# Hybrid attention block: the gated norm's steps placed behind the next heads' scores, and one output gate tile placed ahead of the decays' sums

## The chip, the cores and the metric

The kernel runs on one core of one Trainium2 chip. The metric is the device time of one execution in microseconds (us); of several runs the median is given. TensorE is called PE here (its weight loads PEld), VectorE DVE, ScalarE ACT, GpSimd POOL and SyncE SP.

## The reference, cut to what matters

One layer of an encoder block over 512 positions of 1024 features, in float32: an RMS norm, one wide input projection, two mixers (multi-head latent attention and gated linear attention) that are gated and merged, and then a retrieval of experts by product keys, which takes up most of the time and which the change does not touch. The change touches the gated linear attention (GLA) and the place in the attention (MLA) into which its last steps are woven:

```python
log_a = jax.nn.log_sigmoid((gate_lr @ w_a2 + b_a2).astype(f32)) / GLA_TAU
cum = jnp.cumsum(log_a, axis=2)
cum_last = cum[:, :, -1]
k_dec = kc * jnp.exp(cum_last[:, :, None] - cum)
d_state = jnp.einsum('bclhk,bclhv->bchkv', k_dec, vc)
chunk_decay = jnp.exp(cum_last)
...
o = jnp.einsum('bclhk,cbhkv->bclhv', qc, states)
o = o * lax.rsqrt(jnp.mean(o * o, axis=-1, keepdims=True) + EPS) * g_gn.astype(f32)
o = o.reshape(B, S, H * dv) * jax.nn.silu(out_gate.astype(f32))
```

So each of the 4 GLA heads has decays (sums of log decays and their exponentials), an output that is divided by the root of its mean square (the gated norm), and an output gate. The attention has 8 heads: scores, a masked softmax, and the product with the values.

## The kernel before

Everything is held transposed: features on the 128 partitions, the 512 positions along the row. A product in full precision is made of three matmuls on split operands: high x high, low x high, high x low. A weight tile comes from memory as `raw`; ACT makes its high half `whi`, POOL (some times DVE) its low half `wlo = raw - whi`. The order on every engine is the order in which the program is written (`manual_schedule`); the engines run their own queues and meet at semaphores.

*Decays and gates (lines 536 to 559).* `la` holds the log decays. After two query tiles (`gq`), for each of the 4 blocks of 128 positions PE makes a sum (`pd`, in one of two banks called `pst`), ACT takes its exponential (line 546) and DVE multiplies it onto the keys (`kd`). Then 16 small matmuls give the chunks' totals and ACT their exponentials (`dec`, line 554). Then come 4 output gate tiles: each is 24 matmuls on a weight tile (`proj`, banks `pmm`), a DVE product with the row norm `rX`, and a Silu on ACT (line 559).

*The attention (loop at line 765), heads counted from 0.* One turn `hd` makes the scores of head `hd + 1` (`scores`: 4 matmuls into `pmm` banks; for each, DVE masks, takes the maximum into `stat` and scales it, and ACT takes the exponential into `x`), pieces of gate projections that fill PE's time (`fill`, `piece`: 3 matmuls a piece), the values of head `hd` (`values`: the probabilities of 4 blocks are transposed by PE into two banks called `pk`; DVE copies blocks 0 and 2 out, ACT blocks 1 and 3; then 4 matmuls), and the scaling of head `hd + 1`'s probabilities (`normalise`, DVE).

*The gated norm.* `gla_norm` (in turns 0 and 2, for two heads each) sums the squares by two matmuls; DVE scales the sums into `gsq` (trace name `t`, program name `t_1164`), and ACT makes r = exp(-0.5 ln) (`rB`). A Newton step and the scaling follow for each head: `gla_scale` makes u = -0.5 r r on DVE and u = u x gsq on POOL (line 613) and puts the rest, `gla_scaled`, on a list called `later`: r = (u + 1.5) r on DVE, and the product of the head's output `yb32` (trace name `t`, program name `t_960`) with r on POOL (line 619). `run()` issues all that is on the list. The steps of heads 0 and 1 stand in turns 1 and 2, those of heads 2 and 3 in turns 3 and 4.

Of the kernel before, what the change touches and what calls it, by code (L numbers as in the profile page):

```python
# [16 lines left out]
AF = mybir.ActivationFunctionType  # L17
OP = mybir.AluOpType
# [175 lines left out]
def body(ctx, tc, a, out):  # L194
    nc = tc.nc
    pe, act, dve, pool, sp = (Metered(nc.tensor, _pe_ns), nc.scalar, Metered(nc.vector, _dve_ns), nc.gpsimd, nc.sync)
# [55 lines left out]
    def run(n=1000):  # L252
        for _ in range(n):
            if later:
                later.pop(0)()

    def weights(key):

        while half:
            split_lo()  # L260
        while state["split"] < min(pos_of[key] + 2, len(queue)):
            split_one()
        run(1)
        return ready.pop(key)
# [50 lines left out]
    def pmm(name="pmm"):  # L315
        return ps.tile([128, T], F32, name=name, bufs=4 if name == "pmm" else 2)
# [5 lines left out]
    def tmp(dt=F32, n=T):  # L322
        return tp[0].tile([128, n], dt, name="tmp", bufs=tp[1])
# [80 lines left out]
    def proj(key, xs=None, bank="pmm"):  # L404
        w = weights(key)
        p = pmm(bank)
        acc(p if key[0] != "u" else p[:, GT:], pairs(w, NC_D), xs or hx)
        if key[0] != "u":
            further(key)
        return p  # L410
# [4 lines left out]
    rX = sb.tile([128, T], F32, name="r2")  # L415
# [73 lines left out]
    for c in range(NC_D):  # L489
# [28 lines left out]
        if c >= 3 and c - 3 < NT:  # L518
            tt = c - 3
            p = pmm("pst")  # L520
# [15 lines left out]
    sg, gq = sgq[:, 0:4], sgq[:, 4:6]  # L536
    kd = sb.tile([128, NT, 256], F32, name="kd")
    dec = fr.tile([128, 16], F32, name="dec")
    for i in range(2):
        p = proj(("w1", 6 + i))  # L540
        dve.scalar_tensor_tensor(gq[:, i], p, GDK ** -0.5, rX, op0=OP.mult, op1=OP.mult)
    for tt in range(NT):
        pd = pmm("pst")
        pe.matmul(pd[:, :256], tri, la[:, tt], start=True, stop=True)
        e = tmp(n=256)
        act.activation(e, pd[:, :256], AF.Exp)
        dve.scalar_tensor_tensor(kd[:, tt], pk[tt // 2][:, (tt % 2) * 256:(tt % 2) * 256 + 256], rcol[:, tt:tt + 1], e,
                                 op0=OP.mult, op1=OP.mult)
# [3 lines left out]
            pe.matmul(ptot[:, hp * 8 + 2 * tt:hp * 8 + 2 * tt + 2], la[:, tt, hp * 128:(hp + 1) * 128],  # L552
                      cc(C_IND, 2), start=True, stop=True)
    act.activation(dec, ptot[:, :16], AF.Exp)
    for i in range(4):
        p = proj(("w1", 8 + i))
        t = tmp()
        dve.tensor_tensor(t, p, rX, op=OP.mult)
        act.activation(sg[:, i], t, AF.Silu)


    st = fr.tile([128, 8, 2, 128], F32, name="t2")
# [46 lines left out]
    def gla_scale(hd):  # L609
        r = rg[hd]  # L610
        u = tmp()
        dve.scalar_tensor_tensor(u, r, -0.5, r, op0=OP.mult, op1=OP.mult)
        pool.tensor_tensor(u, u, gsqs[0][:, hd], op=OP.mult)
        later.append(lambda: gla_scaled(hd, u))
# [11 lines left out]
    for g in range(3):  # L626
        w = weights(("wq", g))
        for i in range(2):
            p = pmm()
# [5 lines left out]
            if g < 2:  # L635
                hd = 2 * (2 * g + i)
                act.activation(qT[0:64, hd], p[0:64], AF.Copy)
                dve.tensor_copy(qT[0:64, hd + 1], p[64:128])
            else:

                t, x = tmp(), tmp()
# [7 lines left out]
    for i in range(4):  # L649
        p = pmm()  # L650
# [14 lines left out]
    for tt in range(NT):  # L665
        ts = slice(tt * 128, (tt + 1) * 128)
        p = pmm()
# [13 lines left out]
    def scores(hd):  # L681
        pr = both[:, (hd % 2) * NT:(hd % 2 + 1) * NT]
        st4 = fr.tile([128, 16], F32, name="stat", bufs=3)
        probs[hd] = pr, st4
        for i in range(NT):
            n = (i + 1) * 128
            p = pmm()
            pe.matmul(p[:, :n], qT[0:96, hd, i * 128:n], kT[0:96, hd, :n], start=True, stop=True)
            dve.memset(p[0:64, n - 64:n], -1e30)
            mx, b, sm = (st4[:, 4 * j + i:4 * j + i + 1] for j in range(3))  # L690
            dve.reduce_max(mx, p[:, :n], axis=AX.X)
            dve.tensor_scalar(b, mx, -scale, None, op0=OP.mult)
            act.activation(pr[:, i, :n], p[:, :n], AF.Exp, bias=b, scale=scale, accum_out=sm)
            piece(FS[i] if hd else 0)
# [27 lines left out]
    def fill(n):  # L722
        while half:
            split_lo()
        while gpend:
            i, p = gpend.pop(0)
            t = tmp()
            dve.tensor_tensor(t, p, rX, op=OP.mult)
            sp.dma_start(gated[i], t)
        piece(n)  # L730
# [34 lines left out]
    for hd in range(MH):  # L765
        if hd + 1 < MH:
            scores(hd + 1)
        fill(FILL[1])
        if hd in (0, 2):
            run()  # L770
            gla_norm((hd, hd + 1))
        values(hd)
        if hd + 1 < MH:
            normalise(hd + 1)
        if hd in (1, 3):
            gla_scale(hd - 1)
        fill(FILL[2])
        if hd == 4:
            run()
            yb = [fr.tile([128, 4, T], F32R, name="t3"), fr.tile([128, 4, T], F32R, name="t4")]  # L780
        if hd >= 4:
            split(yb[0][:, hd - 4], yb[1][:, hd - 4], yb32[:, hd - 4], dve)
        elif hd % 2:
            run()
            gla_scale(hd)
        else:
            run()
    while gpend or half:
# [21 lines left out]
    for mt in range(8):  # L810
        g = []
        for s in range(2):
            i = 2 * mt + s
            if i in EARLY:
                t = gin.pop(i)
            else:
                p = proj(("w1", 12 + i))
                t = tmp()
# [6 lines left out]
        for s, y in ((1, yb), (0, ya)):  # L825
            p = pmm()
# [11 lines left out]
    for mt in range(8):  # L838
        p = proj(("wo", mt), mgx)
# [45 lines left out]
    hd = dr.tile([2, 128, D], F32, name="hd")  # L885
# [86 lines left out]
    for mt in range(16):  # L972
# [3 lines left out]
        p = proj(("wpq", mt), h2x)  # L976
# [488 lines left out]
```

## Time and profile before

| | us |
|---|---|
| median of 3 runs | 1633.83 (1633.63 to 1634.84) |
| profiled execution | 1642.5 |
| its span, first to last instruction | 1640.7 |
| PE busy | 1609.1 |
| DVE busy | 1242.6 |
| ACT busy | 728.5 |
| POOL busy | 355.2 |

The profile is one execution. Its rows give, for an instruction or several alike in a row, the start from the beginning of the span, the time it took, the engine, the line, the operation with its output and inputs and, in brackets, how long the engine stood idle before it and which engine's work on which tile ended that wait. Line 161 is that of a helper through which PE and DVE instructions pass; there the tiles tell what an instruction is. The granted clock is PE's, as a share of 2.4 GHz. Busy times of different engines overlap; matmuls of a row overlap too, so that the start of the next row says more than the sum of durations.

### The profile page before, as it was taken

To read this page: it belongs to the slowest core of one execution; us is meant where nothing else is said; L and a number is where in the kernel's file an instruction comes from. 1 tells how busy PE (TensorE), PEld (TensorE's weight loads), DVE (VectorE), ACT (ScalarE), POOL (GpSimd) and SP (SyncE) were. 2 spreads that over 40 slices of the span, in tenths; PEclk is the share of its full clock that TensorE was granted. 3 is DMA by queue.
4 is the path that set the end of the run, shared out by engine and by line. 5 is a ranking of instruction groups with operands and counts; after the bars stand their busy time and mean duration, and the time that the engine had idled before them with its cause. 6 is when DMAs were issued, how large, how long until landed. Compare 5 with 4: busy or idle time off the path is not lost.

```text
span 1640.7 us, 23200 instructions
## 1 busy us (share of the span) xinstructions
PE 1609.1 (98%) x8487; PEld 1399.0 (85%) x8487; DVE 1242.6 (76%) x2513; ACT 728.5 (44%) x1257; POOL 355.2 (22%) x258
## 2 busy tenths in 40 slices
PE   7999999999999999999999999999999999999998
PEld 6777656888889999999999999888888888888776
DVE  6634575343797989889889737787988888988885
ACT  5552544333333645545455544444444434444343
POOL 4342143445354100000001010111111111111110
PEclk9999999999999999999999999999999999999999
DMA  5222112442433678788789898999999999999994
GB/s 170 73 81 77 52 58 90 157 157 90 141 105 128 204 279 291 255 292 309 265 302 350 327 354 291 315 372 344 382 383 356 388 355 377 359 361 367 344 382 151
DMA packets 154610, 415.82 MB, mean 253 GB/s; under 512 B 12343, under 2 KB 87608, under 8 KB 136448
## 3 DMA queue, kind: packets, MB, share of 16 engines
q1 hardware_dynamic: 118048, 230.28, 40.4%
q0 software_dynamic: 19888, 139.23, 22.5%
q10 hardware_dynamic: 16560, 44.83, 7.3%
q8 instruction: 66, 1.08, 0.3%
q14 instruction: 48, 0.39, 0.1%
HBM read 361.60 MB, written 52.17 MB: 252 GB/s over the span
## 4 chain that ended last, share of the span: by engine, by line
PE 85%; issue 4%; DVE 4%; DMA 4%; ACT 1%; POOL 1%; SPq 0%; DVEq 0%; POOLq 0%; ACTq 0%
PE pmm L161 63%; PE pst L161 12%; PE pk L161 10%; DMA ga<-gad 2%; DVE tmp L161 1%; DMA vraw<-in_v 1%; DMA raw<-in_u 1%; POOL wlo L242 1%; DVE t L161 1%; DVE vlo L161 0%; DVE rows L161 0%; DVE rB L161 0%; ACT whi L236 0%; DMA raw<-in_w 0%; DVE gout L161 0%
## 5 line engine op out<-in xcount | busy, mean ns | idle before, releaser
L161 PE MATMUL pmm<-act_hi,whi 128*128 128x384 f32 (+1 forms) x1016 | 362.4, 357 | 9.7 <-ACT act_hi L331 9.3
L161 PE MATMUL pmm<-act_hi,wlo 128*128 128x384 f32 (+1 forms) x1016 | 354.1, 349 | 1.8 <-DVE wlo L161 1.8
L161 PE MATMUL pmm<-act_lo,whi 128*128 128x384 f32 (+1 forms) x1016 | 354.0, 348 | 0.5 <-DVE act_lo L161 0.5
L1023 POOL DMA_INDIRECT rows<-in_uv,gidx x128 | 130.4, 1019 | 889.9 <-DVE gout L161 847.7
L236 ACT ACTIVATE whi<-raw 128x1024 fp32r<-128x1024 f32 (+1 forms) x201 | 209.1, 1042 | 98.8 <-PE pmm L161 52.6
L242 POOL TENSOR_TENSOR wlo<-raw,whi 128x1024 fp32r<-128x1024 f32 (+1 forms) x79 | 186.1, 2360 | 244.8 <-ACT whi L236 234.8
L161 DVE TENSOR_TENSOR wlo<-raw,whi 128x1024 fp32r<-128x1024 f32 x122 | 148.8, 1222 | 88.7 <-ACT whi L236 87.0
L161 PEld LDWEIGHTS pmm<-act_hi,whi 128*128 128x128 f32 x1016 | 192.2, 189 | 24.2 <-ACT act_hi L331 9.3
L161 PEld LDWEIGHTS pmm<-act_hi,wlo 128*128 128x128 f32 x1016 | 192.0, 189 | 11.6 <-DVE wlo L161 2.4
L161 PE MATMUL pmm<-vlo,chi 128*128 128x512 f32 x512 | 200.0, 391 | 1.6 <-DVE vlo L161 1.5
L161 PE MATMUL pmm<-vhi,clo 128*128 128x512 f32 x512 | 199.3, 389 | 1.0 <-DVE clo L161 1.0
L161 PE MATMUL pmm<-vhi,chi 128*128 128x512 f32 x512 | 199.5, 390 | 0.9 <-ACT vhi L1279 0.9
L161 PEld LDWEIGHTS pmm<-act_lo,whi 128*128 128x128 f32 x1016 | 192.4, 189 | 9.0 <-DVE act_lo L161 1.0
L161 DVE SCALAR_TENSOR_TENSOR gout<-rows,gact,gout 128x1024 f32<-128x1024 f32 x128 | 163.9, 1281 | 0.0
L161 DVE TENSOR_TENSOR vlo<-vraw,vhi 128x1024 fp32r<-128x1024 f32 x128 | 156.0, 1219 | 4.4 <-ACT vhi L1279 4.4
L1279 ACT ACTIVATE vhi<-vraw 128x1024 fp32r<-128x1024 f32 x128 | 134.2, 1050 | 49.8 <-DMA vraw<-in_v 49.1
L161 DVE SCALAR_TENSOR_TENSOR rows<-rows,hrep 128x1024 f32<-128x1024 f32 x128 | 155.9, 1218 | 0.0
L161 PE MATMUL pmm<-t,whi 128*128 128x512 f32 x436 | 138.6, 399 | 0.0
L161 PEld LDWEIGHTS pmm<-vlo,chi 128*128 128x128 f32 x512 | 96.1, 188 | 24.3 <-DVE vlo L161 4.5
L1035 ACT ACTIVATE gact<-gact 128x1 f32<-128x1 f32 x128 | 25.9, 202 | 199.1 <-DVE rows L161 198.9
L161 PEld LDWEIGHTS pmm<-vhi,clo 128*128 128x128 f32 x512 | 96.1, 188 | 20.3 <-DVE clo L161 1.5
L161 PEld LDWEIGHTS pmm<-vhi,chi 128*128 128x128 f32 x512 | 96.1, 188 | 19.9 <-ACT vhi L1279 1.3
(276 smaller groups left out, 2785.9 us busy)
## 6 DMA issues: line engine op xcount, KB each, us to landing
raw<-in_u SPq DMA_DIRECT2D x128, 512.0 KB, 5.4
vraw<-in_v SPq DMA_DIRECT2D x124, 512.0 KB, 8.4
gt<-gd SPq DMA_DIRECT2D x30, 768.0 KB, 10.3
gd<-gs ACTq DMA_DIRECT2D x11, 2048.0 KB, 8.1
gad<-gx ACTq DMA_DIRECT2D x96, 192.0 KB, 5.1
ga<-gad SPq DMA_DIRECT2D x95, 192.0 KB, 9.6
raw<-in_w SPq DMA_DIRECT2D x28, 512.0 KB, 3.3
raw<-in_wpq SPq DMA_DIRECT2D x16, 512.0 KB, 3.5
```

The source lines that it names most:

```text
L161: return f(*args, **kw)
L236: act.activation(hi[:, :n], raw[:, :n], AF.Copy)
L242: (lo_eng or lo_home[0]).tensor_tensor(lo[:, :n], raw[:, :n], hi[:, :n], op=OP.subtract)
L1023: pool.indirect_dma_start(out=rows[n], out_offset=None, in_=a["uv"], in_offset=bass.IndirectOffsetOnAxis(ap=gidx[:, n:n + 1], axis=0))
L1035: act.activation(g, g, AF.Gelu)
L1279: act.activation(hi, vraw[n], AF.Copy)
```

## The change

The function `gate_out` holds one output gate tile; tile 0 is now made before the decays' sums and tiles 1 to 3 after them. In the attention, the steps of the gated norm leave the ends of turns 1, 3 (and what remained of them in turns 2 and 4) and stand in turns 2 and 4 right behind the scores of the next head, both heads of a pair at once: `gla_scale`, `run()`, `gla_scale`, `run()`.

```diff
+    def gate_out(i):
+        p = proj(("w1", 8 + i))
+        t = tmp()
+        dve.tensor_tensor(t, p, rX, op=OP.mult)
+        act.activation(sg[:, i], t, AF.Silu)
+
+    gate_out(0)
     for tt in range(NT):
         pd = pmm("pst")
         pe.matmul(pd[:, :256], tri, la[:, tt], start=True, stop=True)
...
     act.activation(dec, ptot[:, :16], AF.Exp)
-    for i in range(4):
-        p = proj(("w1", 8 + i))
-        t = tmp()
-        dve.tensor_tensor(t, p, rX, op=OP.mult)
-        act.activation(sg[:, i], t, AF.Silu)
+    for i in range(1, 4):
+        gate_out(i)
...
         if hd + 1 < MH:
             scores(hd + 1)
+        if hd in (2, 4):
+            gla_scale(hd - 2)
+            run()
+            gla_scale(hd - 1)
+            run()
         fill(FILL[1])
...
         if hd + 1 < MH:
             normalise(hd + 1)
-        if hd in (1, 3):
-            gla_scale(hd - 1)
         fill(FILL[2])
...
             split(yb[0][:, hd - 4], yb[1][:, hd - 4], yb32[:, hd - 4], dve)
-        elif hd % 2:
-            run()
-            gla_scale(hd)
         else:
             run()
```

On ACT at the decays (`kd` is still the log decays' work tile, `x_726` the Silu's output, `tmp<-pst` the exponentials of the sums) the order before is:

```order
L531 ACTIVATE kd<-kd 128x1024
L236 ACTIVATE whi<-raw 128x1024 x2
L546 ACT_TABLE_LOAD
L546 ACTIVATE tmp<-pst 128x256 x4
L554 ACTIVATE dec<-pst 128x16
L236 ACTIVATE whi<-raw 128x1024
L559 ACT_TABLE_LOAD
L559 ACTIVATE x_726<-tmp 128x512
```

and now:

```order
L531 ACTIVATE kd<-kd 128x1024
L236 ACTIVATE whi<-raw 128x1024 x3
L546 ACT_TABLE_LOAD
L546 ACTIVATE x_726<-tmp 128x512
L553 ACT_TABLE_LOAD
L553 ACTIVATE tmp<-pst 128x256 x4
L561 ACTIVATE dec<-pst 128x16
L236 ACTIVATE whi<-raw 128x1024
L546 ACT_TABLE_LOAD
L546 ACTIVATE x_726<-tmp 128x512
```

A Silu with its table stands ahead of the exponentials, and the Silus behind them load their table again.

On DVE, between the maxima of head 3 and the values of head 2, the order is now (with what each row waits for; the last of the maxima is the first row, `tmp<-pmm` is the gate piece's product, `t_1164<-pst` the norm's sums, `t_1569<-pk` the first copy of transposed probabilities):

```order
L161 TENSOR_SCALAR stat<-stat 128x1 [waits DVE_49]
L161 SCALAR_TENSOR_TENSOR tmp<-rB 128x512
L161 SCALAR_TENSOR_TENSOR rB<-tmp,rB 128x512 [waits Pool_49]
L161 SCALAR_TENSOR_TENSOR tmp<-rB 128x512
L161 SCALAR_TENSOR_TENSOR rB<-tmp,rB 128x512 [waits Pool_49]
L161 TENSOR_TENSOR tmp<-pmm,r_119 128x512
L161 TENSOR_SCALAR t_1164<-pst 128x512 [waits PE_49] x2
L161 COPY t_1569<-pk 128x512 [waits PE_49]
```

Before, the first three of these four steps stood ahead of the maxima of head 3, and the fourth between the product and the norm's sums. Head 5's maxima and head 4's values have the same four steps between them now, without a norm's sums; before, the fourth step stood far behind, after head 4's values.

On POOL (line 613 is now 617, 619 is 623) the order before is, from the first step of the norm to the last:

```order
L613 TENSOR_TENSOR tmp<-tmp,t_1164 128x512
L242 TENSOR_TENSOR wlo<-raw,whi 128x1024
L619 TENSOR_TENSOR t_960<-t_960,rB 128x512
L613 TENSOR_TENSOR tmp<-tmp,t_1164 128x512
L619 TENSOR_TENSOR t_960<-t_960,rB 128x512
L242 TENSOR_TENSOR wlo<-raw,whi 128x1024
L613 TENSOR_TENSOR tmp<-tmp,t_1164 128x512
L242 TENSOR_TENSOR wlo<-raw,whi 128x1024
```

and now:

```order
L617 TENSOR_TENSOR tmp<-tmp,t_1164 128x512
L623 TENSOR_TENSOR t_960<-t_960,rB 128x512
L617 TENSOR_TENSOR tmp<-tmp,t_1164 128x512
L623 TENSOR_TENSOR t_960<-t_960,rB 128x512
L242 TENSOR_TENSOR wlo<-raw,whi 128x1024 x2
L617 TENSOR_TENSOR tmp<-tmp,t_1164 128x512
```

The weight splits no longer stand between the steps of a pair.

## Rows read from the trace of the kernel before

**Rows 1.** The page, first part: busy us, share of the span, instructions.

```profile
PE 1609.1 (98%) x8487; PEld 1399.0 (85%) x8487; DVE 1242.6 (76%) x2513; ACT 728.5 (44%) x1257; POOL 355.2 (22%) x258
```

**Rows 2.** Stretches: length, then busy us of each engine, PE's granted clock, DMA.

```profile
95.00:120.00 25.00, 24.04 (x99) 19.49 (x99) 5.74 (x10) 12.53 (x16) 9.53 (x4) 0.86 0.22 72
150.00:175.00 25.00, 24.07 (x119) 19.13 (x117) 13.75 (x22) 7.04 (x13) 2.35 (x1) 0.80 0.19 56
175.00:250.00 75.00, 70.65 (x295) 45.92 (x294) 51.44 (x133) 36.57 (x81) 25.42 (x14) 1.00 0.17 60
300.00:320.00 20.00, 20.00 (x89) 16.42 (x88) 4.83 (x7) 5.21 (x7) 9.63 (x4) 1.00 0.25 82
```

**Rows 3.** Order of time, PE: decays' sums, and outputs of GLA heads 0 and 1.

```profile
100.73 1.03 PE L161 MATMUL pst<-la,tri 128*128 128x256 f32 x4
102.68 1.13 PE L161 MATMUL pst<-la,tri 128*128 128x256 f32 x4 [0.92 <-ACT tmp L546]
...
156.49 0.69 PE L161 MATMUL pk<-x,t 64*128 64x64 f32 x2 [0.94 <-DVE t L161]
```

**Rows 4.** Order of time, ACT: exponentials of the decays, and a later Silu.

```profile
100.95 1.28 ACT L546 ACT_TABLE_LOAD   x1
102.24 0.66 ACT L546 ACTIVATE tmp<-pst 128x256 f32<-128x256 f32 x2
...
120.78 0.63 ACT L559 ACTIVATE x<-tmp 128x512 f32<-128x512 f32 x1 [3.86 <-DVE tmp L161]
```

**Rows 5.** Order of time, POOL: low halves of gate tiles 0 and 1.

```profile
100.06 4.77 POOL L242 TENSOR_TENSOR wlo<-raw,whi 128x1024 fp32r<-128x1024 f32 x2 [6.23 <-ACT whi L236]
```

**Rows 6.** Order of time, DVE: the product of a gate tile.

```profile
120.06 0.69 DVE L161 TENSOR_TENSOR tmp<-pmm,r 128x512 f32<-128x512 f32 x1 [4.75 <-PE pmm L161]
```

**Rows 7.** Order of time, PE: last score matmul of heads 2, 3 and 5.

```profile
198.83 1.13 PE L161 MATMUL pmm<-big,big 96*128 96x512 f32 x2 [0.17 <-ACT x L693]
...
211.52 1.13 PE L161 MATMUL pmm<-big,big 96*128 96x512 f32 x2 [1.09 <-ACT x L693]
...
238.93 1.12 PE L161 MATMUL pmm<-big,big 96*128 96x512 f32 x2 [1.12 <-ACT x L693]
```

**Rows 8.** Order of time, DVE: u, r, products, norm's sums, first copy.

```profile
204.81 0.69 DVE L161 SCALAR_TENSOR_TENSOR tmp<-rB 128x512 f32<-128x512 f32 x1
206.87 2.87 DVE L161 SCALAR_TENSOR_TENSOR rB<-tmp,rB 128x512 f32<-128x512 f32 x1 [1.38 <-POOL tmp L613]
...
213.67 0.68 DVE L161 TENSOR_TENSOR tmp<-pmm,r 128x512 f32<-128x512 f32 x1
214.27 0.68 DVE L161 SCALAR_TENSOR_TENSOR rB<-tmp,rB 128x512 f32<-128x512 f32 x1
214.87 1.28 DVE L161 TENSOR_SCALAR t<-pst 128x512 f32<-128x512 f32 x2
...
241.08 0.68 DVE L161 TENSOR_TENSOR tmp<-pmm,r 128x512 f32<-128x512 f32 x1
241.68 0.68 DVE L161 COPY t<-pk 128x512 f32<-128x512 f32 x1
```

**Rows 9.** Order of time, POOL: the norm's steps and a weight split.

```profile
205.57 1.26 POOL L613 TENSOR_TENSOR tmp<-tmp,t 128x512 f32<-128x512 f32 x1 [9.22 <-DVE tmp L161]
206.79 2.39 POOL L242 TENSOR_TENSOR wlo<-raw,whi 128x1024 fp32r<-128x1024 f32 x1
209.82 1.64 POOL L619 TENSOR_TENSOR t<-t,rB 128x512 f32<-128x512 f32 x1 [0.63 <-DVE rB L161]
```

**Rows 10.** Order of time, PE: transposes and values of heads 2 and 4.

```profile
217.06 0.38 PE L161 MATMUL pk<-cst,x 128*128 128x128 f32 x2
...
220.96 1.54 PE L161 MATMUL pst<-t,t 128*64 128x384 f32 x6 [0.29 <-ACT t L753]
...
242.75 0.49 PE L161 MATMUL pk<-cst,x 128*128 128x128 f32 x3
```

**Rows 11.** Order of time, ACT: table load of the norm's logarithm, turn 2.

```profile
215.63 1.28 ACT L605 ACT_TABLE_LOAD   x1 [1.06 <-DVE t L161]
```

## Prediction

> **What bounds the kernel now.** I read the page first: TensorE (PE) is busy for 98% of the span [rows 1], so only what lengthens or shortens PE's own row of work moves the end, and a microsecond lost anywhere on PE is a microsecond at the end. The matmuls of the changed places lie between 95 and 250 us of the span; the stretch table there shows where PE loses time: it idles for parts of a microsecond, and its granted clock falls twice [rows 2]. Then I read the order of time on each engine at the three places that the diff touches. A level of 0.50 is 1.2 GHz, a level of 1.00 is 2.4 GHz.
>
> At the decays' sums, PE comes from the second query tile straight into the sums at 100.73 us: that row shows no idle time ahead of it. Then it waits 0.92 us before the second pair of sums, because their bank is free only when ScalarE (ACT) has taken an exponential, and ACT first loads a table [rows 3, 4]. In the attention the scores of heads 3 and 5 each show a wait of 1.09 and 1.12 us before their last matmul, where head 2 (nothing of the gated norm ahead of it) waits 0.17 us [rows 7]. The cause is on VectorE (DVE): u, r and the next u of the norm stand there in front of the scores' maxima, and r alone took 2.87 us because the weight split `wlo` held GpSimd (POOL) at the same time [rows 8, 9].
>
> **Part 1, the gate tile ahead of the sums.** It adds no matmul; it moves 24 matmuls, one DVE product and one Silu, and ACT loads one table more (Silu, Exp, Silu in place of Exp, Silu). No wait for `la` is there to be hidden, since PE has none at 100.73 us. Two waits appear instead.
>
> First, the weights. A gate tile takes 0.69 + 4.75 = 5.44 us of PE at full clock (from one DVE product to the next, [rows 6]), 0.227 us for each of its 24 matmuls. Its third matmul needs the low half of its weights. POOL waits for ACT's high halves and makes the low halves of this and the next tile in 4.77 us from 100.06 us, so the first is there at 100.06 + 4.77 / 2 = 102.45 us [rows 5]. PE would want it at 100.73 + 2 x 0.227 = 101.18 us. It waits 1.27 us. So far the sums stood in this gap.
>
> Second, ACT's table. The other 22 matmuls end near 102.45 + 22 x 0.227 = 107.45 us, some 0.15 us later in the bank. The product takes 0.69 us, the Silu starts 0.72 us after the product's start and takes 0.63 us [rows 6, 4]: done near 108.95 us. The Exp table follows the Silu on ACT: 1.28 us, until 110.25 us. In the kernel before, the second pair of sums starts 0.44 us after the exponential does (102.68 - 102.24), so now near 110.7 us. The first pair, 1.03 us long [rows 3], ends at 108.5 us. PE idles 2.2 us in place of 0.92 us: 1.3 us more. The extra Silu load comes under the next tile's matmuls and costs nothing there (5.44 us of cover; without it 1.28 us). Part 1 gives 1.27 + 1.3 = **2.6 us later**. Bounds: 0, if weights and table were both ready, and one table load more, 3.9 us.
>
> The Trainium skill (ScalarE: Activation LUTs, What ACT_TABLE_LOAD costs) says that each switch of a table set costs a drain of about 1380 ns beside the 1283 ns of the load. By that PE would idle about 1.4 us longer still. The row of the load agrees with the 1283 ns, but the exponential behind it starts 0.01 us after the load's end [rows 4]; I leave the drain out.
>
> **Part 2, the norm behind the scores.** It removes u, r, u from the front of the maxima of heads 3 and 5. The gain is the two long waits less the ordinary one: 0.92 + 0.95 = 1.87 us of PE [rows 7].
>
> What it adds is a ping-pong between two engines with nothing in between. Each pair of heads is now scaled in one go: DVE u, POOL tmp, DVE r, DVE u, POOL t, POOL tmp, DVE r, and DVE works in order, so the pieces behind it (the gate tile's product, the norm's sums, the copies of the transposed probabilities) stand still while POOL works. In the kernel before, the first r waited for POOL in the same way, but the second r had the twelve steps of the maxima between itself and its u. The length from the rows, counted from the moment the maxima are done: u 0.69; POOL starts 0.07 later and takes 1.26; r starts 0.04 later and takes 0.68 (the 2.87 falls away, no weight split stands between any more); POOL's t starts 0.07 later and takes 1.64 beside DVE's second u, which it covers; tmp 1.26; r starts 0.04 later, and the next DVE row begins 0.60 after r [rows 8, 9]. Sum: 0.69 + 1.33 + 0.72 + 1.71 + 1.26 + 0.64 = 6.35 us.
>
> Head 2's values (scores of head 3 ahead). The maxima end at 213.67 in the rows, 0.92 earlier without the long wait: 212.75. Plus 6.35 is 219.1 for the gate tile's product, 0.60 later for the norm's first sum: 219.7, where it started at 214.87 [rows 8]. That is 4.8 us later. Two things hang on it. The third block's transposes need the bank that the first copy frees; that copy now ends near 221.6, and PE, which would have come there at 217.06 - 0.92 = 216.1, idles about 5.4 us [rows 10]. And ACT's table load for the logarithm waits for the norm's sum (its row names DVE's t), and behind it on ACT stand logarithms, exponentials and the copy for which the second matmul of the values waits [rows 11, 10]. That chain set PE's time already and slides by 4.8 us whole. PE ends **4.8 us later**, the gain included.
>
> Head 4's values. The maxima would end at 241.08 - 0.95 = 240.13; plus 6.35 is 246.5 for the product, 247.1 to 247.8 for the first copy (0.60 later, 0.68 long, as the rows at 241.08 and 241.68). The last transpose waits for that copy. It started at 242.95 (the third of the row at 242.75) and now starts at 247.8 [rows 8, 10]. PE ends **4.85 us later**, after an idle time of 5.8 us. POOL's last pass and the weight splits behind it come later too, and a split is wanted only about 5 us after, so I cost that at nothing; without that cover it would be one split's 2.39 us.
>
> Bounds of part 2: POOL's t took 1.64 us beside DVE but could be as short as its tmp, 1.26 us, so 0.4 us less each. Upwards I know of no row longer than the ones used except r's 2.87 us; once in each place that is 2.2 us more each.
>
> **The clock.** The two falls in the trace came behind idle times of 0.92 and 0.94 us among small matmuls [rows 3]. The first cost 25 x 0.14 = 3.5 us, the second 25 x 0.20 = 5.0 us [rows 2]. Idle times of 5.4 and 5.8 us are several times as long. Each may bring one fall, for a cost between nothing (the half clock falls into time in which PE waits anyway) and 3.5 us; I take 1.5 us each, **3 us** together, the middle being nearest for a fall of which the first part is idle. The first fall stays: the thin stretch of sums is as long as before.
>
> The Trainium skill (TensorE: Matmul & The Clock Gate, Part 1) says that the default is the low clock and that idleness brings it back. By that a fall after each of the two long waits is certain, and the sum is nearer its upper end.
>
> **The sum.** 2.6 + 4.8 + 4.85 + 3 = 15.25 us later. In the stretches behind, as at 300 us, PE is busy throughout [rows 2] and has no reserve that would swallow it. The profiled execution took 1642.5 us (1640.7 of span), the timed runs 1633.83 us in the median, 0.5% less; the difference is carried over whole: 1633.83 + 15.2 = **1649.0 us**, and some 1657.7 us for a profiled execution.
>
> **The rivals.**
> (a) Stalls without new falls of the clock: 1633.83 + 12.25 = 1646 us. For it: the waits of 1.09 and 1.12 us lie in a stretch at 1.00 [rows 2]. Against it: none was so long.
> (b) The falls spread: each new one costs its 3.5 us in full, and the second of the old ones, 2.6 us later now among the same small matmuls, grows by more than half, 3 us: 1633.83 + 12.25 + 7 + 3 = 1656 us. For it: the second fall was already longer than the first. Against it: part of each new fall lies in idle time.
> (c) Not slower: the waits behind the scores are covered. The place is the bank of the transposes. PE comes there 216.1 - 212.75 = 3.4 us behind the maxima of head 3 and 242.0 - 240.13 = 1.9 us behind those of head 5; product, sums and copy take 0.60 + 1.20 + 0.68 = 2.5 us of the one, product and copy 1.3 us of the other. So the ping-pong is hidden as long as it takes under 0.9 and 0.6 us. Then the 1.87 us gained would stay, and with part 1 at its lower bound it is 1632 us (1628 us if the first fall of the clock, 3.5 us, went as well). Against it stand 6.35 us in rows, of which 4.16 us are POOL's passes alone.
> (d) The change does not do what it says, so that nothing moves: 1634 us. Against it: the rows of DVE, ACT and POOL stand in the new order.
>
> **Chances.** Forecast (1649) 0.55; (a) 0.22; (b) 0.14; (c) 0.05; (d) 0.04. A measurement of this kernel tells 0.2% (3.3 us) from no change. Faster by more than that needs (c) with a fall of the clock gone as well: 0.03; within 0.2%: 0.05; slower: 0.92. The range, 1641 to 1657 us: below, both parts at their lower bounds and no fall (0 + 9.65 - 0.8 = 8.9 us) with part of a fall saved; above, (b).
>
> **What would show it.** The waits of PE should have a new first row: the transposes (`pk`) waiting for DVE, about 5 us the longest, one at each of the two places, with the granted clock under 1.00 behind them. The scores of heads 3 and 5 should wait about 0.17 us. On DVE each second-half r should wait for POOL 1.4 and about 2.3 us. Near 101 us PE should wait about 1.3 us for POOL's `wlo`, near 108.5 us about 2.2 us for ACT. If the transposes do not wait, or the norm's DVE steps are taken up by another bank being free, the prediction is wrong; if only the clock stays up, (a).

## The result and the profile after

The changed kernel takes **1652.83 us** in the median (4 runs, 1651.09 to 1657.05), the kernel before 1634.34 us (4 runs beside it): 18.5 us more, a ratio of 1.0114 with a 95% interval of 1.0088 to 1.0139. It is slower, as forecast, and 3.8 us slower than the forecast. In all, the kernel before was run 95 times, with a median of 1635.8 us; against these the change costs 17.0 us, so some 1.5 of the 18.5 us come from the four runs of the kernel before beside it.

PE's order of time at the places of [rows 3, 7, 10], with the same columns (start, duration, engine, line, operation, count, and in brackets the idle time and what ended it):

```profile
102.09 0.50 PE L161 MATMUL pmm<-act_hi,wlo 128*128 128x512 f32 x1 [1.25 <-POOL wlo L242]
...
107.23 1.03 PE L161 MATMUL pst<-la,tri 128*128 128x256 f32 x4
110.53 1.13 PE L161 MATMUL pst<-la,tri 128*128 128x256 f32 x4 [2.27 <-ACT tmp L553]
...
206.79 1.47 PE L161 MATMUL pmm<-big,big 96*128 96x128 f32 x6
208.43 1.13 PE L161 MATMUL pmm<-big,big 96*128 96x512 f32 x2 [0.17 <-ACT x L697]
...
219.46 0.69 PE L161 MATMUL pk<-cst,x 128*128 128x128 f32 x2 [5.32 <-DVE t L161]
...
229.29 1.47 PE L161 MATMUL pmm<-big,big 96*128 96x128 f32 x6
...
242.69 1.12 PE L161 MATMUL pmm<-big,big 96*128 96x512 f32 x2 [0.17 <-ACT x L697]
...
252.54 0.48 PE L161 MATMUL pk<-cst,x 128*128 128x128 f32 x1 [5.65 <-DVE t L161]
```

Two new waits stand at the decays (1.25 and 2.27 us; before one of 0.92), and two at the transposes of heads 2 and 4 (5.32 and 5.65 us). The waits of 1.09 and 1.12 us in the scores of heads 3 and 5 [rows 7] are now 0.17 us each. DVE behind the maxima of head 3, against [rows 8]:

```profile
210.58 0.68 DVE L161 SCALAR_TENSOR_TENSOR tmp<-rB 128x512 f32<-128x512 f32 x1
212.65 0.69 DVE L161 SCALAR_TENSOR_TENSOR rB<-tmp,rB 128x512 f32<-128x512 f32 x1 [1.39 <-POOL tmp L617]
213.26 0.68 DVE L161 SCALAR_TENSOR_TENSOR tmp<-rB 128x512 f32<-128x512 f32 x1
216.32 0.69 DVE L161 SCALAR_TENSOR_TENSOR rB<-tmp,rB 128x512 f32<-128x512 f32 x1 [2.38 <-POOL tmp L617]
216.93 0.68 DVE L161 TENSOR_TENSOR tmp<-pmm,r 128x512 f32<-128x512 f32 x1
217.53 1.28 DVE L161 TENSOR_SCALAR t<-pst 128x512 f32<-128x512 f32 x2
218.72 0.68 DVE L161 COPY t<-pk 128x512 f32<-128x512 f32 x1
```

From the first u (210.58) to the gate tile's product (216.93) DVE does nothing but the four steps, and waits for POOL in two of them; the copy that frees the bank for the third block's transposes comes only at 218.72. ACT, against [rows 4, 11]:

```profile
108.15 0.63 ACT L546 ACTIVATE x<-tmp 128x512 f32<-128x512 f32 x1 [5.47 <-DVE tmp L161]
108.80 1.28 ACT L553 ACT_TABLE_LOAD   x1
110.09 0.66 ACT L553 ACTIVATE tmp<-pst 128x256 f32<-128x256 f32 x2
...
218.29 1.28 ACT L609 ACT_TABLE_LOAD   x1 [6.81 <-DVE t L161]
```

Silu, table and exponential follow one another without a gap, and the logarithm's table is loaded at 218.29, where it was loaded at 215.63 in a turn that began 2.17 us later: 4.83 us later in its turn. The stretches, with the columns of [rows 2] (the granted clock is the third number from the end):

```profile
95.00:120.00 25.00, 21.43 (x94) 17.05 (x93) 5.69 (x9) 13.39 (x17) 9.53 (x4) 0.93 0.26 82
...
150.00:175.00 25.00, 24.03 (x132) 18.17 (x130) 15.47 (x30) 9.64 (x15) 2.35 (x1) 0.93 0.18 58
...
200.00:225.00 25.00, 18.99 (x68) 11.34 (x68) 13.52 (x33) 10.74 (x21) 8.12 (x6) 0.88 0.11 42
225.00:250.00 25.00, 21.54 (x92) 13.93 (x90) 12.81 (x35) 8.46 (x22) 7.95 (x5) 0.98 0.16 53
250.00:275.00 25.00, 22.11 (x83) 13.83 (x84) 16.55 (x40) 7.00 (x19) 6.52 (x4) 0.86 0.18 63
```

Behind each long wait the granted clock is under 1.00, where it was at 1.00 between 175 and 250 us [rows 2]. The length of a turn is read from the first score rows of heads 3, 4, 5 and 6. After, they start at 206.79, 229.29, 241.05 and 260.58 us. Of the kernel before, PE's order of time:

```profile
208.96 1.47 PE L161 MATMUL pmm<-big,big 96*128 96x128 f32 x6
...
224.62 1.47 PE L161 MATMUL pmm<-big,big 96*128 96x128 f32 x6
...
236.35 1.47 PE L161 MATMUL pmm<-big,big 96*128 96x128 f32 x6
...
249.04 1.47 PE L161 MATMUL pmm<-big,big 96*128 96x128 f32 x6
```

Turn 2 takes 22.50 us where it took 15.66, and turn 4 takes 19.53 us where it took 12.69: 6.84 us more in each. Turn 3 between them is the same (11.76 and 11.73).

The two profiled executions differ by 9.6 us of span only (1650.3 and 1640.7). Most of the reason is in the two old falls of the clock: 3.5 + 5.0 = 8.5 us in the profile of before [rows 2], 25 x 0.07 = 1.75 us each here, although the waits at the sums are longer and the wait ahead of the second is the same (0.92 us). The falls differ from run to run. The runs list the mean granted clock of each, so a clock loss, (1 - clock) x span, can be worked out for every run (the clock is given to 0.001, 1.6 us, so only means of several runs say much, and a low clock inside a wait is counted though it costs nothing). The standard error of the mean clock loss, from the spread of the runs, is 0.4 us for the kernel before and 0.5 to 2.2 us for the others. All kernels of this study, over all their runs (the versions are described below):

| kernel | runs | median | mean | mean clock loss | mean time less loss |
|---|---|---|---|---|---|
| before | 95 | 1635.8 | 1636.2 | 6.0 | 1630.2 |
| after | 4 | 1652.8 | 1653.4 | 13.6 | 1639.8 |
| gate tile alone | 10 | 1641.4 | 1642.4 | 9.7 | 1632.7 |
| norm alone | 5 | 1647.7 | 1649.2 | 10.5 | 1638.6 |
| after, zero matmuls in the waits | 4 | 1654.7 | 1654.9 | 9.5 | 1645.4 |
| after, u u r r | 4 | 1650.4 | 1652.2 | 15.3 | 1636.9 |
| gate tile ahead, Silu late | 12 | 1638.1 | 1640.6 | 8.9 | 1631.7 |
| gate tile between the sums | 12 | 1634.2 | 1634.2 | 4.5 | 1629.7 |
| the same, empty entry | 12 | 1639.8 | 1639.1 | 8.9 | 1630.2 |
| the same, norm split | 12 | 1636.6 | 1637.4 | 8.9 | 1628.5 |
| the same without the entry | 12 | 1634.6 | 1633.9 | 6.0 | 1627.9 |
| early states | 12 | 1631.4 | 1632.2 | 4.2 | 1628.0 |
| early states, norm as after | 12 | 1645.7 | 1645.7 | 9.5 | 1636.3 |
| early states, turn 4 as after | 13 | 1640.0 | 1640.0 | 7.2 | 1632.8 |

The change adds 9.6 us of time without clock loss and 7.6 us of clock loss; the forecast had 12.25 and 3. A part of the difference is only in the counting, since the second of the new falls begins inside its wait (in the profile at about 250.0 us, and the wait ends at 252.54, which makes some 1.3 us of loss that cost nothing). How much of the rest is real is the question for the experiments.

### The profile page after: what moved, and what is told of

It reads as the page before. It is cut to its first block, busy times and chain, and to the rows that moved or that the text cites. A ratio compares the mean times of both kernels' runs of the same rounds, so it can differ in the third digit from the quotient of the medians.

```text
span 1650.3 us, 23200 instructions
## 1 busy us (share of the span) xinstructions
PE 1608.9 (97%) x8487; PEld 1397.0 (85%) x8487; DVE 1241.8 (75%) x2513; ACT 729.7 (44%) x1258; POOL 354.9 (22%) x258
## 4 chain that ended last, share of the span: by engine, by line
PE 85%; DVE 5%; DMA 5%; issue 2%; ACT 2%; POOL 1%; SPq 0%; ACTq 0%; DVEq 0%; POOLq 0%
PE pmm L161 62%; PE pst L161 12%; PE pk L161 11%; DMA ga<-gad 3%; DMA vraw<-in_v 2%; DVE tmp L161 1%; DVE rB L161 1%; DVE vlo L161 1%; DVE rows L161 1%; POOL wlo L242 0%; DVE t L161 0%; DMA raw<-in_w 0%; POOL tmp L617 0%; ACT act_hi L331 0%; DVE stat L161 0%
```

## The experiments

**The two parts apart.** The gate tile alone (the diff's first two pieces):

> The kernel before with only the first part of the change: output gate tile 0 ahead of the decays' sums, the gated norm in its old place. My theory: PE waits about 1.3 us for the low half of the tile's weights and about 2.3 us (0.92 before) for ACT's exponentials behind the Silu's table, so 2.6 us later than before, +0.16%; a fall of the clock at another place moves that by up to 3.5 us either way. Rival (the loss lies in the gate tile, the norm's place is harmless): +15 us or more. Rival (the gate tile brings a gain that the norm eats): faster than before by 1 us or more.

Measured 1641.41 us, ratio 1.0046 (1.0024 to 1.0068): +7.3 us in place of +2.6. Its profile, PE's order of time:

```profile
101.74 0.50 PE L161 MATMUL pmm<-act_hi,wlo 128*128 128x512 f32 x1 [1.26 <-POOL wlo L242]
...
110.21 1.13 PE L161 MATMUL pst<-la,tri 128*128 128x256 f32 x4 [2.27 <-ACT tmp L553]
```

The waits are those of the forecast to 0.1 us, and the mean time without clock loss rises by 2.5 us. The mean clock loss rises by 3.7 us (standard error 1.4), which the forecast doesn't have; rival (b) has 3 us of it. In the stretches of this profile:

```profile
95.00:120.00 25.00, 21.43 (x87) 17.06 (x86) 5.58 (x9) 13.02 (x16) 9.57 (x4) 0.86 0.26 76
...
150.00:175.00 25.00, 24.08 (x113) 18.75 (x111) 14.21 (x24) 6.36 (x11) 2.96 (x2) 0.73 0.20 60
```

The first fall is as long as before (0.86), the second, 50 us behind the edit, longer (0.73, before 0.80). One profile of each doesn't settle in which of the two stretches the 3.7 us lie in the mean.

The norm alone (the rest of the diff):

> The kernel before with only the second part: the steps of the gated norm behind the next heads' scores, the gate tiles in their old place. My theory: PE stands 5.3 and 5.7 us before transposes, with a fall of the clock behind each; 1650 us, that is +16 us against before (9.65 us of waits and some 6 us of clock). Rival without a share of the clock: +9.7 us. Rival (the gate tile is the cause): no more than 3 us from before.

Measured 1647.74 us, ratio 1.0082 (1.0056 to 1.0108): +13.6 us, less than the 16 expected and a little over the 4.8 + 4.85 + 3 = 12.65 of the prediction's terms for this part. The two parts add up, 7.3 + 13.6 = 20.9 against 18.5, within the spread of the runs.

**Can PE's waits be filled?** In the changed kernel, matmuls by zeros stand in the two long waits; they add nothing to an open sum.

```diff
+PADS = {(2, 2): 22, (4, 3): 23}
...
+    def idle_pad(n):
+        for _ in range(n):
+            pe.matmul(opened[0][0:64], zero, hx[0][0], start=False, stop=False, skip_group_check=True)
...
+            if (hd, j) in PADS:
+                idle_pad(PADS[hd, j])
```

> The changed kernel with PE kept busy in the two long waits: 22 matmuls that add zeros to an open gate tile before the third block's transposes of head 2, 23 before the last transpose of head 4 (0.227 us each, 5.0 and 5.2 us, a little less than the waits). The waits of the other engines stay as they are; only PE's idleness goes. My theory (idle time takes the clock down, and the clock costs about 3 us behind each wait): the granted clock stays at 1.00 there and the time is 5 to 7 us less than that of the changed kernel. Rival (the clock is not the cause, all of the loss is the waits): within 1 us of the changed kernel.

Measured 1654.69 us, ratio 1.0117 (1.0083 to 1.0151): no gain where 5 to 7 us were expected. PE in turns 2 and 4:

```profile
215.44 5.25 PE L162 MATMUL pmm<-act_hi,zero 128*64 128x512 f32 x22
220.98 0.44 PE L162 MATMUL pk<-cst,x 128*128 128x128 f32 x2 [0.29 <-DVE t L162]
225.14 0.48 PE L162 MATMUL pk<-cst,x 128*128 128x128 f32 x1 [3.72 <-ACT t L769]
...
251.03 5.52 PE L162 MATMUL pmm<-act_hi,zero 128*64 128x512 f32 x23
257.01 0.33 PE L162 MATMUL pk<-cst,x 128*128 128x128 f32 x1 [0.45 <-DVE t L162]
```

Turn 4 is what the experiment was to be: the wait is filled, the granted clock is 1.00 in each five microseconds from 245 to 265 us, and the turn takes 17.70 us (245.44 to 263.14), 1.83 us less than in the changed kernel. There, in one profile, the wait is worth 17.70 - 12.69 = 5.0 us and the clock 1.8 us. Turn 2 was spoilt: the last transposes wait 3.72 us for ACT's copy, where in the changed kernel they wait 0.52 us for DVE's, and the turn takes 25.46 us. So the total says nothing on the clock; turn 4 alone does.

**What the ping-pong's order costs.** In the changed kernel, both u first, then both r:

```diff
             gla_scale(hd - 2)
-            run()
             gla_scale(hd - 1)
             run()
```

> The changed kernel with the two heads of a pair interleaved: u, u on DVE, then both of POOL's products, then r, r, in the same place behind the scores. My theory (the length is the hand-over to and fro, in which POOL's output pass of the first head stands between): from the end of the maxima to the gate piece's product 4 to 5 us in place of 6.37 us, so 1.4 to 2.4 us less at each of the two places and 3 to 5 us in the whole. Rival (the place alone counts, not the order of the steps in it): no change against the changed kernel.

Measured 1650.37 us, ratio 1.0111 (1.0065 to 1.0156), 2.5 us under the changed kernel (3 to 5 expected), with intervals that overlap. The trace is clearer, PE's order of time:

```profile
219.14 0.44 PE L161 MATMUL pk<-cst,x 128*128 128x128 f32 x2 [3.71 <-DVE t L161]
...
249.34 0.47 PE L161 MATMUL pk<-cst,x 128*128 128x128 f32 x1 [4.00 <-DVE t L161]
```

Both waits are 1.6 us shorter, one pass of POOL's t (1.64 us in [rows 9]), which no longer stands between the two r. That pass stood in the wait with its full length.

**The place of the gate tile.** From the kernel before, the tile ahead of the sums with its Silu behind the last exponential (`gate_out` now returns the Silu as a function, which is called later); then the tile between the second and the third sum, its Silu there too:

```diff
+    silu = gate_out(0)          # first kernel
     for tt in range(NT):
+        if tt == 2:             # second kernel
+            silu = gate_out(0)
         pd = pmm("pst")
...
     act.activation(dec, ptot[:, :16], AF.Exp)
+    silu()
```

> The kernel before with gate tile 0 ahead of the decays' sums, but its Silu behind the last exponential (dec), so that ScalarE goes straight to the Exp table while the tile runs. It keeps the wait for the low half of the weights (1.27 us) and takes away the wait for Silu, table and exponential (2.27 us between the pairs of sums). Theory (the tile in front costs waits, and the clock's loss grows with the length of the wait among the small matmuls): TensorE waits 1.3 us for wlo, under 0.6 us between the pairs of sums, and the time is +1.3 - 0.92 + 0.4 = about +0.8 us against before, the mean clock loss near before's: about 1635 us, 5 us under the run with the gate tile alone. Rival (the loss of clock there comes from the new order itself, a longer low stretch behind the tile, and not from the wait): the clock loss stays as with the gate tile alone, 1639 to 1641 us.

Measured 1638.07 us, ratio 1.0031 (1.0005 to 1.0057). The 12 runs fall into two groups: seven of 1632 to 1638 us at a mean clock of 0.995 to 0.999, five of 1645 to 1650 us at 0.990 or 0.991. The wait between the pairs of sums is gone from the trace and the time without clock loss is 1.0 us less than with the gate tile alone (1.8 expected), but the mean clock loss, 8.9 us, is not clearly lower (standard error 1.7, and 1.3 for the gate tile alone). Neither theory holds whole: the wait for the Silu costs time, but without it the clock loss doesn't go back to that of the kernel before. What sets the two groups apart isn't shown; the kept profile is of a run of the faster group (1635.99 us).

> The kernel before with gate tile 0 between the second and the third of the four decays' sums, its Silu behind dec. The tile then stands where TensorE waited 0.92 us. Theory: the sums' bank is free long before the tile ends, the third matmul of the tile comes 0.45 us behind the second sum and wlo is there at about 102.45 us, so TensorE waits under 0.4 us in place of 0.92: -0.6 us of waits, and if the first fall of the clock came from that wait, up to 3.5 us more: 1630 to 1634 us. Rival (falls come from the run of small matmuls whatever the waits): the granted clock of 95 to 120 us stays about 0.86 and the time is that of before less 0.6 us.

Measured 1634.16 us, ratio 0.9992 (0.9974 to 1.0010). Its first wait in PE's order of time:

```profile
101.98 0.50 PE L161 MATMUL pmm<-act_hi,wlo 128*128 128x512 f32 x1 [0.38 <-POOL wlo L242]
```

0.38 us for `wlo` in place of 1.25, no wait between the sums, and the clock loss is 4.5 us, half that of the kernel before this one. What differs between the two is two sums and the wait for `wlo`. Both losses have large standard errors (0.9 and 1.7 us). And a fall is in this profile, too, without a wait ahead of it:

```profile
108.17 1.95 PE L161 MATMUL pst<-cst,la 128*128 128x2 f32 x16
...
110.00:115.00 5.00, 5.00 (x17) 3.97 (x17) 0.00 (x0) 3.04 (x4) 1.69 (x1) 0.66 0.01 3
```

PE was busy for 4.96 of the 5 us before 110 us, the last 1.8 of them with the 16 small matmuls of the chunks' totals; from 111.3 to 114.3 us its matmuls then start 0.43 us apart in place of 0.23, at the lower clock. So a fall at the decays doesn't need a wait, and the rival holds in part; the fall is half as long as in the profile of before (0.93 from 100 to 125 us, before 0.86).

**A wait moved.** Behind the states of the gated linear attention, PE waits 0.94 us at 156 us [rows 3]. An empty entry ahead of the outputs, in the version with the tile between the sums:

```diff
-... for c in range(8)] + [lambda hd=hd: gla_out(hd)
+... for c in range(8)] + [lambda: None] + [lambda hd=hd: gla_out(hd)
```

> As the last one, and the first output of the gated linear attention stands one product later (an empty entry ahead of it in the list that is woven into the query and key products), so that the state that it reads is finished when TensorE comes. It takes away the wait of 0.94 us at 156 us. Theory: without a wait there the second fall of the clock (25 us at 0.80, 5.0 us in the profile of before) does not come: 0.9 us of wait and 1 to 5 us of clock, 1627 to 1632 us, the granted clock of 150 to 175 us at 1.00. Rival: the wait goes elsewhere or the fall comes anyway: 0 to 0.9 us less than the last one.

Measured 1639.76 us, ratio 1.0006 (0.9985 to 1.0027), a miss. PE, and the granted clock of the stretch:

```profile
159.82 3.07 PE L161 MATMUL pk<-x,t 64*128 64x64 f32 x16 [2.18 <-DVE t L161]
```

The wait has moved and grown. DVE's own order shows why:

```profile
153.40 4.85 DVE L161 TENSOR_TENSOR big<-tmp 32x512 f32<-32x512 f32 x4
...
159.01 1.41 DVE L161 SCALAR_TENSOR_TENSOR t<-pk,cst,x 128x512 f32<-128x512 f32 x2
```

The outputs' products `t<-pk`, which free PE's bank, now stand behind four sums into `big` that took 4.85 us. The profile gives this stretch (150 to 175 us) a clock of 0.73, and the runs lose 8.9 us where they lost 4.5. A wait added by mistake is a test as well: 1.25 us more of wait (0.93 before), 4.4 us more of clock loss (standard error 1.3). The next version keeps the entry and splits the norm: both u at the end of turns 1 and 3, both r behind the next heads' maxima (in turn 4 behind the values):

```diff
         if hd in (1, 3):
             gla_scale(hd - 1)
+            gla_scale(hd)
...
-        elif hd % 2:
-            run()
-            gla_scale(hd)
-        else:
+        elif hd % 2 == 0:
             run()
```

> As the last one, and of the gated norm both u of a pair (DVE and POOL) stand at the end of turns 1 and 3, both r only behind the next heads' maxima (in turn 4 behind the values). No DVE step then waits for POOL in front of anything that TensorE needs. Theory: two steps of 0.68 us instead of 5.6 us stand ahead of the maxima, the waits of 1.09 and 1.12 us of the scores fall to about 0.2 us; in turn 2 the second r adds 0.68 us behind the maxima, of which some 0.3 to 0.5 us show at the third block's transposes; so -1.9 + 0.5 = -1.4 us against the last one, and no fall of the clock between 200 and 275 us. Rival (DVE is late anyway and the wait comes back behind the scores): 0 +- 0.5 us against the last one.

Measured 1636.65 us, ratio 1.0001 (0.9985 to 1.0018). Turn 2 takes 15.37 us, turn 4 11.76: 1.2 us less together than before (1.4 expected), and the clock is at 1.00 from 200 to 275 us. Without the empty entry:

> The last one (gate tile between the sums, both u of a pair early and both r late) without the empty entry, which had brought a wait of 2.18 us at 160 us in place of the one of 0.94 us: the first output of the gated linear attention stands where it stood before. Theory (waits cost, and each wait of more than about 1 us among the small matmuls brings a fall of the clock in more of the runs): mean clock loss as with the gate tile between the sums alone, 4.5 us, time without the loss 1629.7 - 1.5 = 1628.2 us; together 1632 to 1634 us, about 3 us under before. Rival (the loss of clock does not go by the waits): loss as in the last one, 8.9 us, 1637 us.

Measured 1634.63 us, ratio 0.9993 (0.9973 to 1.0012); clock loss 6.0 us, nearer to 4.5 than to 8.9, but with a standard error of 1.3 us that hardly tells them apart. Then the empty entry with the first two states made together, so that the outputs stand where they stood:

```diff
-[lambda c=c: gla_state(c) for c in range(8)] + [lambda: None]
+[lambda: (gla_state(0), gla_state(1))] + [lambda c=c: gla_state(c) for c in range(2, 8)] + [lambda: None]
```

> As that with the empty entry, but the first two chunks' states are made together, so that the last state stands one product earlier and the empty entry keeps the outputs where they stood before. The wait of 0.94 us at 156 us goes without any other step's place changing. No wait of more than 0.55 us is then left on TensorE between 95 and 270 us. Theory: 0.9 us of wait less than the one before it and hardly any fall of the clock: loss 0.5 to 3 us, time without it 1627.5 us, together 1628 to 1631 us, and the granted clock of 150 to 175 us at 1.00. Rival (small matmuls alone bring the falls): the loss stays at 4 to 6 us, 1632 us or more.

Measured **1631.38 us, ratio 0.9973 (0.9950 to 0.9995)**: 0.3% under the kernel before, with an interval that ends just short of 1. Its stretches:

```profile
95.00:120.00 25.00, 24.58 (x116) 20.07 (x115) 6.33 (x10) 13.17 (x17) 11.42 (x5) 1.00 0.26 81
150.00:175.00 25.00, 23.52 (x122) 18.24 (x122) 19.16 (x37) 11.27 (x22) 4.74 (x2) 1.00 0.19 59
200.00:225.00 25.00, 23.47 (x95) 14.03 (x94) 15.24 (x45) 13.47 (x29) 8.44 (x6) 1.00 0.19 64
225.00:250.00 25.00, 24.65 (x109) 16.56 (x109) 18.30 (x44) 9.73 (x25) 11.28 (x6) 1.00 0.24 84
```

No fall is left in this profile before 1575 us. But the edit didn't remove the wait: one of 1.01 us now stands at 160 us. The mean loss of 4.2 us is more than the 0.5 to 3 expected and lies where the rival had it, and the mean time less loss is that of the version before it (1628.0 and 1627.9).

**The long waits by themselves.** On this last version, the norm in the changed kernel's order, in both turns and in turn 4 alone:

> The version with the early states and the gate tile between the sums, with the gated norm in the changed kernel's order: its two long waits are now the only ones of their kind between 95 and 270 us, so their price in clock stands by itself. Against that version the waits alone should add 5.1 us in turn 2 and 5.8 us in turn 4 (time less clock loss 1639 us). Clock: 1.5 us for each wait, as the prediction has it, gives 1646 us; 2.3 us for each, as the kernel with the norm alone had it, 1647.5 us; whole falls of 3.5 us, 1650 us. Rival (the falls of the changed kernel came from the older short waits and are only moved by the long ones): no loss more than the 4.2 us of the version without, 1643 us.

> As the last one, but with the changed order in turn 4 alone; turn 2 keeps the split order (both u early, both r late). One wait of about 5.7 us. Waits alone: +5.8 us, 1634 us without clock loss. If each long wait has its own fall, the clock loss lies halfway between the version without a long wait (4.2 us) and the last run, so 1640 us; if one wait is enough to bring all of the loss, the loss is that of the last run, 1642 us or more.

Measured 1645.67 us, ratio 1.0056 (1.0036 to 1.0076), and 1640.01 us, 1.0023 (1.0006 to 1.0040). Turn 4 alone adds 8.6 us in the median and 7.8 in the mean, both turns 14.3 and 13.6. The clock loss goes from 4.2 to 7.2 to 9.5 us: 3.0 for one wait, 2.3 for the other (standard error 0.9 each), some of it inside the waits, so that the times less loss, 1636.3 and 1632.8, lie under the 1639 and 1634 expected. Each wait has its own fall, and the long waits don't merely move older ones: in both profiles the clock is at 1.00 from 95 to 175 us. PE's rows of the first of the two, the same waits as in the changed kernel, with the first score rows of heads 3 to 6:

```profile
199.26 1.47 PE L161 MATMUL pmm<-big,big 96*128 96x128 f32 x6
...
211.93 0.69 PE L161 MATMUL pk<-cst,x 128*128 128x128 f32 x2 [5.32 <-DVE t L161]
...
221.88 1.46 PE L161 MATMUL pmm<-big,big 96*128 96x128 f32 x6
...
233.65 1.47 PE L161 MATMUL pmm<-big,big 96*128 96x128 f32 x6
...
245.14 0.47 PE L161 MATMUL pk<-cst,x 128*128 128x128 f32 x1 [5.64 <-DVE t L161]
...
253.22 1.47 PE L161 MATMUL pmm<-big,big 96*128 96x128 f32 x6
```

The turns give the price of the clock without the part inside the waits. Turn 2 takes 22.62 us and turn 4 19.57; less the turns of the kernel before and the 4.8 and 4.85 us of the prediction's waits, 2.2 and 2.0 us are left. The changed kernel gives 2.0 and 2.0, the norm alone (22.14 and 19.35 us) 1.7 and 1.8, turn 4 of the second kernel here (19.43 us) 1.9.

Five microseconds each around and behind the end of the wait in turn 4 of the second (237.22 us):

```profile
235.00:240.00 5.00, 2.78 (x7) 1.93 (x7) 4.69 (x8) 0.80 (x2) 3.84 (x3) 0.50 0.14 52
240.00:245.00 5.00, 5.00 (x18) 2.88 (x18) 1.31 (x3) 0.00 (x0) 0.00 (x0) 0.87 0.28 105
```

The clock is at its lower level, 1.2 GHz, when the wait ends, and comes back within the next stretch.

## Why the prediction was right, and where it was off

**Part 1, the weights:** 1.27 us forecast, 1.25 measured. **The table:** an idle time of 2.2 us forecast, 2.27 measured, with Silu, load and exponential at 108.15, 108.80 and 110.09 where the working had them end near 108.95 and 110.25. The Trainium skill (ScalarE: Activation LUTs, What ACT_TABLE_LOAD costs) would add a drain of about 1380 ns; the exponential starts 0.01 us behind the load's end here too, so leaving it out was right.

**Part 2, the chain:** 6.35 us forecast from the maxima to the product, 216.93 - 210.58 = 6.35 measured (6.37 in turn 4). The waits of PE: 5.4 and 5.8 us forecast, 5.32 and 5.65 measured. The gain in the scores, 1.87 us, came (0.17 us is left of each wait). The logarithm's table load named DVE's t, as expected. POOL's late splits cost nothing that the rows show. That POOL's passes stand in the waits with their length was shown by taking one away: 1.6 us less. By turns, 4.8 + 1.5 and 4.85 + 1.5 = 12.65 us were forecast with the clock, and 13.7 measured.

**The clock is the term that was mis-sized.** For the two long waits 1.5 us each were taken, between nothing and 3.5; the seven turns with such a wait give 1.7 to 2.2, turn 4 with its wait filled 1.8. That makes some 4 us in place of 3. The working took the first part of each fall as idle. In turn 4 this is so, as shown above; in turn 2 the fall of the changed kernel begins at about 219.2 us, when the wait ends (219.46), and lasts until 226 us, 3.4 us of loss by the clock, of which the turn shows 2.0. The Trainium skill (TensorE: Matmul & The Clock Gate, Part 1), by which idleness brings the low clock back, agrees on the fall behind each long wait; that a fall is certain and that its price is the full 3.5 us are two things.

The other clock term is the sentence "The first fall stays: the thin stretch of sums is as long as before", a term of zero that asked how long the thin stretch is, and not how long PE waits there; one wait of 0.92 us had become two of 1.25 and 2.27. By the mean of its runs the gate tile alone lost 3.7 us more to the clock, and 2.6 us forecast for part 1 became 6.2. So the term was too small there. For the changed kernel this isn't shown: its mean lies 17.2 us over that of the kernel before, of which 13.7 are the two turns and 2.6 the waits of part 1, so that 0.9 us is left for all other falls, less than the 1.3 us to which four runs give the mean. What the waits do at the sums, and what lies at 156 us, stays open, as does why one order lost 8.9 us in the mean as runs of two kinds.

So the direction and the waits were right by their mechanism. Of the 3.3 us between the forecast change and the measured one, 1.5 lie in the runs of the kernel before, 1.0 in the clock of the two turns, and the rest is within the noise.

**The rivals.** (a), no new falls, is refuted by the rows behind both waits. (b), falls that spread, had too high a price for the new ones (3.5 us each). That the second old fall grows, its other part, isn't shown: from 150 to 175 us the four profiles with the tile and its Silu ahead have a clock of 0.93, 0.73, 1.00 and 1.00, the two with the old order 0.80 and 1.00. The result, 1652.8, lies between the forecast and (b). (c) and (d) are refuted by the waits of 5.32 and 5.65 us. The profiled execution was forecast at 1657.7 us and took 1652.07: the difference between a profile and the runs was carried over as if it were a constant, and for the most part is how long the clock fell in one execution.

## What to carry to other kernels

Steps that hand a tile back and forth between two in-order engines are as long as the passes of both, one after the other, and everything queued behind them waits for that long: put the first halves ahead of other work and the second halves behind it, so that the passes lie beside it, as the split norm does. On an engine that is busy for 98% of the time, a new wait costs its length and a share of clock, and the share should be read from the granted clocks of many runs, since one profile can show a fall three times as long as another with the same wait, or none. Before an entry is inserted to hide one wait, look at what it pushes the next steps behind: here a wait of 0.94 us became one of 2.18 us.

## What the runs showed of the hardware

The kernel before, run 95 times, lies between 1628.8 and 1645.8 us; with time drawn against clock loss, one microsecond of loss is 0.96 us of time, and three quarters of the variance of the times go with PE's clock.

Where falls begin, all fourteen profiles tell. Each of the ten waits of 3.7 to 5.7 us has one, which begins inside the wait or within 1.1 us of its end. Behind shorter waits it differs: with the wait of 0.9 us at 156 us, four of nine profiles have a fall (the stretch of 150 to 175 us at 0.73 twice, 0.80 and 0.93, the others at 1.00), with the 2.18 us of the empty entry both, with 1.01 us at 160 us none of three, and the ten waits of 1.09 to 1.12 us in the scores none. At the decays the fall begins beside or behind the 16 small matmuls or the last sums, with or without a wait:

| order at the decays | longest waits of PE, us | granted clock of 100 to 125 us, by profile | mean loss, us |
|---|---|---|---|
| as before | 0.92 | 0.86, 0.93 | 2.6 |
| tile ahead with its Silu | 1.25 and 2.27 | 0.93, 0.86, 0.80, 0.80 | 3.8 |
| tile ahead, Silu late | 1.25 | 0.93 | 1.8 |
| tile between the sums | 0.38 | 0.93, 1.00, 0.93, 0.93, 1.00, 1.00, 1.00 | 0.8 |

The waits there seem to lengthen the fall, but they are not its only cause, and a few profiles of each order don't give the price.

A weight split on POOL slows DVE's two-input steps beside it, as r in [rows 8] already showed (2.87 us beside `wlo`, 0.69 in the changed kernel without one). DVE's four sums into `big` show it again: in the kernel before they took 2.78 us with POOL idle,

```profile
152.56 2.78 DVE L161 TENSOR_TENSOR big<-tmp 32x512 f32<-32x512 f32 x4
```

and 4.85 us with the empty entry, where a split ran from 154.18 us on:

```profile
154.18 2.84 POOL L242 TENSOR_TENSOR wlo<-raw,whi 128x1024 fp32r<-128x1024 f32 x1 [10.32 <-PE pmm L161]
```
